# Where the adaLN rows stand on VectorE, which tiles have how many buffers, and when bank reads and residual loads are issued, in a hybrid RWKV-7 decoder block

## The chip, the cores and the metric

The kernel runs on one core of a Trainium2 chip. The core has five engines that run side by side, each with its own queue of instructions taken in order: TensorE (PE; its weight loads are listed apart as PEld) for matrix products, VectorE (DVE) and ScalarE (ACT) for elementwise work, GpSimd (POOL), and SyncE (SP), whose queue here issues all the transfers between device memory and on-chip memory. The metric is the device time of one execution in microseconds (us).

## The reference

One decoder layer on x of 512 tokens by 2048 features, in float32. The adaLN vector c gives six modulation rows of 2048 numbers each: shift, scale and gate for each of the two halves of the layer.

```python
c_act = jax.nn.silu(c)
mod = c_act @ w_ada[l] + b_ada[l]
sh1, sc1, gt1, sh2, sc2, gt2 = jnp.split(mod[:, None, :], N_MOD, axis=-1)
h = _rmsnorm(x, norm1_g[l]) * (1.0 + sc1) + sh1
p = h @ w_in[l]
y_rwkv = _rwkv7_mixer(p[..., :N_RWKV_COLS], ...)
y_pool = _pool_mixer(p[..., N_RWKV_COLS:], pool_w[l], pool_b[l], pool_scale[l])
mix = jnp.concatenate([y_rwkv, y_pool], axis=-1) @ w_out[l]
x = x + gt1 * mix
h = _rmsnorm(x, norm2_g[l]) * (1.0 + sc2) + sh2
x = x + gt2 * _conv_ffn(h, w_up[l], conv_w[l], conv_b[l], w_down[l])
return _rmsnorm(x, norm_f_g)
```

The RWKV-7 mixer first blends each token's projection with the one before it (`p + mu * (shift(p) - p)`), makes decay, in-context rate and gate from three small LoRA products, and then runs, for each of 16 heads of 64 features, a recurrence over the 512 tokens: the state S is decayed, corrected by a delta rule and read out. The result is normalised per head, gets a bonus term, and is multiplied by the gate g. The pooling mixer takes running means over windows of 2, 4, 8 and 16 tokens and a 256 by 256 product for each of its four groups.

## The kernel before, in words

All activations lie transposed, features on the 128 partitions and the 512 tokens along the free axis. A large product is made in three passes: weights and activations are each split into a high and a low half that TensorE can take at full rate (`split_weights`, lines 117 to 125: ScalarE writes `whi`, VectorE writes `wlo`; four buffers for the raw weights, three for each half), and high by high, high by low and low by high are added in PSUM (lines 128 to 130).

A framework orders the instructions when the program is built: it takes what is ready by an estimate of time, the block with the highest priority first, and the order of each engine's queue is then fixed. At run time an instruction waits for what it needs, and what stands behind it on its engine waits with it. `hp()` and `tc.high_priority` lift a block; everything else has the order of the program text. `in_step(op, other)` adds an edge without a semaphore: `op` is placed behind `other` in the planned order, and nothing waits at run time.

The stages that matter here, in order:

- First projection: adaLN rows 0 to 31 and the input projection of nine tiles (up to about 205 us). Eight banks of PSUM, `pf[0..7]`, hold the last eight of its results. `shift` (line 267) reads a bank twice: ScalarE scales it into a tile (line 268) and VectorE adds the neighbour token's share (line 269). `xwa` (the LoRA inputs for decay and rate) gets a tanh (line 282), `xg` (two tiles of gate input) a sigmoid and a split into halves (lines 288 to 295), and then five banks give r, k, v of the first heads. The pool of the eight banks is closed, and its banks go to the next stage's tiles, each as soon as its reader is done.
- Four quads (`NQ`), each of four heads, 64 tokens by 64 tokens in chunks of `C = 64`. `front(g)` (lines 406 to 460) makes decay and rate; `rest(g)` (from line 462) makes the scores of each chunk (lines 483 and 485, and 542 and 544), inverts the 16 by 16 diagonal blocks on VectorE after a round trip through device memory (lines 507 to 572, the last VectorE operation at 566), then widens the inverse in two levels (lines 586 to 605: product, mask `pm` at 591, product, sum into X at 599, product, sum into Y at 605), then runs the eight chunks of the recurrence one after the other (lines 620 to 650; R at 624 and 625), reads out y (line 668), normalises it (675 to 680) and applies the gate with weights loaded as `lg` and split into `gw` (lines 683 to 693).
- As filler between the quads' own steps stand the projections of the next quads' r, k and v (`win_some`: a product of 48 matmuls, then `shift` into a tile `spill` that goes to device memory, lines 703 to 711) and the pooling groups (`pool`, from line 312; its weights are loaded by `load_pw` into a tile of the tag `war`).
- adaLN rows 32 to 79, cut in two halves along the 2048 inputs: 96 rows of 128 by 1024 (`ada_rest`, lines 372 to 386). Each is a load of 512 KB into a tile `war` with two buffers (line 380) and one VectorE operation that multiplies by silu(c) and sums (line 381). 24 rows belong to each quad; each is placed in step with a filler product (`beats`, a list of the last matmul of each weight tile), spread evenly over the filler of that quad, and the last 24 over the first pass of w_out.
- w_out, first pass (lines 765 to 782): 14 of the 16 tiles of the mixers' output are loaded back (`mxl`, line 767, in the buffers of the raw weights), split, and multiplied for the first ten output tiles; the sums go to device memory as `part`. Then the stage's memory is given up.
- w_out, second pass (from line 866): the residual tiles `x2` are loaded, ten from `part` and six from x, all 16 in one loop ahead of the products (lines 867 to 870). For the first ten output tiles the last two mixer tiles are added; the other six are made whole, in two halves of the tokens. `residual` (line 821) scales by the gate, adds, and sums squares for the second norm.
- The MLP, the down projection and the final norm, which the change does not touch.

Of the kernel before, what the change touches and what calls it, by code (L numbers as in the profile page):

```python
# [11 lines left out]
F32 = mybir.dt.float32  # L12
# [6 lines left out]
P = 128  # L19
T = 512  # L20
# [44 lines left out]
def block_kernel(ctx, tc, a, out, stop=None, dbg=None):  # L65
# [121 lines left out]
    if True:  # L187
# [78 lines left out]
        if True:  # L266
# [15 lines left out]
            S.activation(xwa[0:64, :], xwa[0:64, :], AF.Tanh)  # L282
            xg = two(cell("X", "xg"))
            xgh = []
            for i in range(2):
                t = xg[:, i, :]
                shift(pf[1 + i], 25 + i, t)
                S.activation(t, t, AF.Sigmoid)
                hi = ra.tile([P, T], F32R, tag=f"xgh{i}", name=f"xgh{i}")
                S.copy(hi, t)  # L290
                xgh.append(hi)
            xg1h, xg2 = xgh
            xg1l = ra.tile([P, T], F32R, tag="xg1l", name="xg1l")
            V.tensor_tensor(xg1l, xg[:, 0, :], xg1h[:, :].bitcast(F32), op=ALU.subtract)
            V.tensor_tensor(xg2[64:96, :], xg[64:96, 1, :], xg2[64:96, :].bitcast(F32), op=ALU.subtract)

            RKV = ("R", "K", "V")
            rkv0 = [cell(RKV[i], "rkv"[i]) for i in range(3)]
            for i, (t, x, m) in enumerate(((0, 0, 0), (1, 0, 8), (2, 0, 16), (0, 1, 1), (1, 1, 9))):
                shift(pf[3 + i], m, two(rkv0[t])[:, x, :])  # L300
            ps0ctx.close()
# [10 lines left out]
    def pool(gi):  # L312
# [18 lines left out]
        for d in range(2):  # L331
            ps = mmtile()
            for i in range(2):
                pe = PE.matmul(ps, pw[:, i, d * P : (d + 1) * P], z[:, i, :], start=i == 0, stop=i == 1)
# [35 lines left out]
    modq = ra.tile([P, 2, 48], F32, tag="modq", name="modq")  # L370

    def ada_rest(n0, n1):
        b, at = len(beats) - first_beat[0], first_beat[0]
        for n in range(n0, n1):
# [4 lines left out]
            wa = ra.tile([P, 2 * T], F32, tag="war", name="war", bufs=2)  # L379
# [17 lines left out]
    def flat(t):  # L397
        return t[:, 0 : 2 * T]
# [7 lines left out]
    def front(g, rkv):  # L406
# [31 lines left out]
        V.tensor_sub(cs, cs, mid[:, :, :].to_broadcast([P, 2 * NK, C + 1]))  # L438
# [14 lines left out]
        V.tensor_scalar_max(flat(inv), wide(psn), 1e-24)  # L453
# [813 lines left out]
```

## Time and profile before

| | us |
|---|---|
| median of 3 runs | 2329.66 |
| lowest and highest run | 2323.95 and 2334.65 |
| the profiled execution | 2332.65 |
| its span, first to last instruction | 2330.9 |

The profile is of one execution. Its page gives the busy time of each engine, the span in slices, the chain of work that ended last, the costliest groups of instructions and the transfers. Other views group instructions by line or tile, list who waited for whom, count busy time within given stretches, or list instructions in order of time. In a line such as `L381 DVE ... war<-war,cq x96 | 116.9, 1220 | 47.3 <-DMA war<-ada 47.2` stand the source line, the engine, the output and inputs by the program's names, the count, the total busy time in us and the mean in ns, and then how long the engine stood idle just before, and for what.

### The profile page before, as it was taken

How to read it: one execution, taken by the hardware profiler on the slowest of the kernel's cores; microseconds unless marked ns; L12 is line 12 of the kernel's file. 1: busy time of each engine (PE TensorE's matmuls, PEld its weight loads, DVE VectorE, ACT ScalarE, POOL GpSimd, SP SyncE). 2: the span in 40 equal slices, each digit the busy share in tenths (PEclk: the TensorE clock that was granted, in tenths of full speed). 3: DMA queues.
4: the chain of work that ended last, by engine and by line, in shares of the span. 5: the costliest groups of instructions: out<-in, count | busy, mean ns of one | idle time of the engine just before them, and what ended most of it. 6: DMA issues, size and time to landing. Idle time of an engine off the chain costs nothing.

```text
span 2330.9 us, 41813 instructions
## 1 busy us (share of the span) xinstructions
PE 2202.7 (95%) x16306; PEld 1878.0 (81%) x16306; DVE 1512.6 (65%) x2536; ACT 925.9 (40%) x1551; POOL 403.3 (17%) x390
## 2 busy tenths in 40 slices
PE   7999898888879898999999999999999999999997
PEld 5776666565657798899999999999999788888887
DVE  7896767685865669776656666656666444464457
ACT  4435242332523255544344434443444333343333
POOL 0000000000000005634434333344343000000000
PEclk9999999999989999999999999999999999999999
DMA  9884556566655775433333333333333766666555
GB/s 348 301 307 132 164 181 184 166 202 197 209 177 171 266 224 166 149 108 119 123 109 123 109 115 112 110 117 122 109 122 105 232 202 200 198 199 205 163 165 177
DMA packets 197465, 401.41 MB, mean 172 GB/s; under 512 B 37521, under 2 KB 49553, under 8 KB 193041
## 3 DMA queue, kind: packets, MB, share of 16 engines
q1 hardware_dynamic: 197266, 398.73, 54.0%
q8 instruction: 128, 2.10, 0.4%
q14 instruction: 71, 0.58, 0.1%
HBM read 364.56 MB, written 34.09 MB: 171 GB/s over the span
## 4 chain that ended last, share of the span: by engine, by line
PE 60%; DVE 2%; DMA 2%; ACT 0%; issue 0%; SPq 0%; DVEq 0%; ACTq 0%
PE b L130 20%; PE b L128 20%; PE b L129 20%; DVE wlo L124 1%; DMA wraw<-wdn 1%; DMA wraw<-wout 1%; DVE hl L159 0%; DVE x L1089 0%; ACT whi L122 0%; DVE acc L819 0%; DMA ald<-actd 0%; DVE h L157 0%; DMA x<-part 0%; DMA x<-x2d 0%; DVE x L823 0%
## 5 line engine op out<-in xcount | busy, mean ns | idle before, releaser
L122 ACT CAST whi<-wraw 128x512 fp32r<-128x512 f32 (+1 forms) x594 | 360.4, 609 | 820.8 <-DMA wraw<-wup 254.8
L124 DVE TENSOR_TENSOR wlo<-wraw,whi 128x512 fp32r<-128x512 f32 (+1 forms) x578 | 406.5, 705 | 270.9 <-ACT whi L122 263.1
L128 PE MATMUL b<-ah,whi 128*128 128x512 f32 (+1 forms) x980 | 350.0, 357 | 8.2 <-ACT whi L122 7.3
L130 PE MATMUL b<-ah,wlo 128*128 128x512 f32 (+1 forms) x980 | 349.5, 357 | 6.0 <-DVE wlo L124 5.8
L129 PE MATMUL b<-al,whi 128*128 128x512 f32 (+1 forms) x980 | 348.7, 356 | 0.0
L130 PE MATMUL b<-hh,wlo 128*128 128x512 f32 (+1 forms) x640 | 237.8, 372 | 6.0 <-DVE wlo L124 5.8
L128 PE MATMUL b<-hh,whi 128*128 128x512 f32 (+1 forms) x640 | 238.2, 372 | 0.0
L129 PE MATMUL b<-hl,whi 128*128 128x512 f32 (+1 forms) x640 | 237.8, 372 | 0.0
L128 PEld LDWEIGHTS b<-ah,whi 128*128 128x128 f32 x980 | 186.0, 190 | 36.6 <-ACT whi L122 10.8
L130 PEld LDWEIGHTS b<-ah,wlo 128*128 128x128 f32 x980 | 186.0, 190 | 34.4 <-DVE wlo L124 7.7
L129 PEld LDWEIGHTS b<-al,whi 128*128 128x128 f32 x980 | 186.1, 190 | 26.0
L984 DVE TENSOR_TENSOR pl<-raw,ph 128x768 fp32r<-128x768 f32 x104 | 105.4, 1014 | 153.0 <-ACT ph L983 153.0
L128 PE MATMUL mm<-ah,whi 128*128 128x512 f32 x444 | 183.3, 413 | 10.1 <-ACT whi L122 10.1
L130 PE MATMUL mm<-ah,wlo 128*128 128x512 f32 x444 | 183.8, 415 | 3.2 <-DVE wlo L124 3.2
L129 PE MATMUL mm<-al,whi 128*128 128x512 f32 x444 | 182.4, 411 | 0.0
L972 POOL TENSOR_TENSOR sums<-sums,raw 128x256 f32<-128x256 f32 x104 | 107.5, 1033 | 417.0 <-DVE sl L984 411.1
L130 PE MATMUL b<-tk,sl 128*128 128x256 f32 x624 | 176.7, 283 | 0.0
L129 PE MATMUL b<-tk,sh 128*128 128x256 f32 x624 | 176.5, 283 | 0.0
L128 PE MATMUL b<-tk,sh 128*128 128x256 f32 x624 | 176.0, 282 | 0.0
L983 ACT CAST ph<-raw 128x768 fp32r<-128x768 f32 x104 | 86.3, 830 | 165.9 <-PE b L129 159.5
L381 DVE SCALAR_TENSOR_TENSOR war<-war,cq 128x1024 f32<-128x1024 f32 x96 | 116.9, 1220 | 47.3 <-DMA war<-ada 47.2
L971 POOL TENSOR_TENSOR sums<-raw 128x512 f32<-128x512 f32 x104 | 135.8, 1305 | 66.9 <-DMA raw<-wups 33.1
(277 smaller groups left out, 4699.8 us busy)
## 6 DMA issues: line engine op xcount, KB each, us to landing
raw<-wups SPq DMA_DIRECT2D x104, 512.0 KB, 3.5
war<-ada SPq DMA_DIRECT2D x96, 512.0 KB, 4.4
wraw<-wdn SPq DMA_DIRECT2D x192, 256.0 KB, 3.2
wraw<-wup SPq DMA_DIRECT2D x160, 256.0 KB, 3.6
wa<-ada SPq DMA_DIRECT2D x32, 1024.0 KB, 7.5
wraw<-win SPq DMA_DIRECT2D x108, 256.0 KB, 4.1
ald<-actd SPq DMA_DIRECT2D x88, 256.0 KB, 2.7
wraw<-wout SPq DMA_DIRECT2D x78, 256.0 KB, 4.2
```

The source lines that it names most:

```text
L122: mark[0] = S.copy(hi[:, 0:w], raw[:, 0:w]).ins
L124: mark[1] = eng.tensor_tensor(lo[:, 0:w], raw[:, 0:w], hi[:, 0:w].bitcast(F32), op=ALU.subtract).ins
L128: PE.matmul(ps, wh, xh, start=start, stop=False)
L129: PE.matmul(ps, wh, xl, start=False, stop=False)
L130: return PE.matmul(ps, wl, xh, start=False, stop=stop)
L381: op = V.scalar_tensor_tensor(wa, wa, 1.0, cq[0], op0=ALU.mult, op1=ALU.mult, accum_out=modq[:, kq, j : j + 1])
L971: G.tensor_tensor(sa, raw[:, 1:3, :], raw[:, 0:1, :].to_broadcast([P, 2, W2]), op=ALU.add)
L972: G.tensor_tensor(sb2[:, 0, :], sa[:, 0, :], raw[:, 2, :], op=ALU.add)
L983: act = S.copy(hi[:, sl, :], t)
L984: dve = V.tensor_tensor(lo[:, sl, :], t, hi[:, sl, :].bitcast(F32), op=ALU.subtract)
```

## The change

The 24 rows of a quad are no longer placed in step with filler products. Each quad now collects in a list `spots[g]` 25 of its own VectorE operations, some of them twice or four times, and `ada_rest` places one row behind each of the first 24: three in `front` (lines 438, 453 and 458), two behind the scores of line 485, two behind those of line 544, four behind the end of the block inversion (line 566), one behind each mask (line 591), one behind each of the seven R sums (line 625), two behind the sum of line 668, one behind line 677 and up to two behind line 680. The last 24 rows stand behind quad 3's operations. The tile `war` gets three buffers. `spill`, `lg` and R get one buffer in place of two, and the pool weights, loaded in two halves, take the tags `lg` and `gw`. The eight `shift`s come first, with the tanh behind the fourth; the sigmoids, their casts and the low halves come behind all eight. The loads of the residual tiles go into the loops, each behind the product that it belongs to.

```diff
             shift(pf[0], 24, xwa)
-            S.activation(xwa[0:64, :], xwa[0:64, :], AF.Tanh)
             xg = two(cell("X", "xg"))
...
+            for i in range(2):
+                shift(pf[1 + i], 25 + i, xg[:, i, :])
+            for i, (t, x, m) in enumerate(((0, 0, 0), (1, 0, 8), (2, 0, 16), (0, 1, 1), (1, 1, 9))):
+                shift(pf[3 + i], m, two(rkv0[t])[:, x, :])
+                if i == 0:
+                    S.activation(xwa[0:64, :], xwa[0:64, :], AF.Tanh)
+            ps0ctx.close()
+            xgh = [ra.tile([P, T], F32R, tag=f"xgh{i}", name=f"xgh{i}") for i in range(2)]
...
+            def sigmoids():
+                for i in range(2):
+                    S.activation(xg[:, i, :], xg[:, i, :], AF.Sigmoid)
+                    S.copy(xgh[i], xg[:, i, :])
+                V.tensor_tensor(xg1l, xg[:, 0, :], xg1h[:, :].bitcast(F32), op=ALU.subtract)
+                V.tensor_tensor(xg2[64:96, :], xg[64:96, 1, :], xg2[64:96, :].bitcast(F32), op=ALU.subtract)
+
+            sigmoids()
 
     def load_pw(gi):
-        t = ra.tile([P, 2 * T], F32, tag="war", name="pw", bufs=2)
-        pw = t[:, 0:T].rearrange("p (i d) -> p i d", i=2)
-        nc.sync.dma_start(pw, a["poolw"][gi, :, :, :])
+        pw = [ra.tile([P, 2, P], F32, tag="lg", name="pw"), ra.tile([P, 3, P], F32, tag="gw", name="pw")[:, 0:2, :]]
+        for i in range(2):
+            nc.sync.dma_start(pw[i], a["poolw"][gi, :, i, :].rearrange("p (d w) -> p d w", d=2))
         return pw
...
+    spots = [[] for _ in range(NQ)]
 
     def ada_rest(n0, n1):
-        b, at = len(beats) - first_beat[0], first_beat[0]
-        for n in range(n0, n1):
+        for n, spot in zip(range(n0, n1), spots[n0 // 24]):
             kq, j = divmod(n, 48)
...
-            wa = ra.tile([P, 2 * T], F32, tag="war", name="war", bufs=2)
+            wa = ra.tile([P, 2 * T], F32, tag="war", name="war", bufs=3)
             nc.sync.dma_start(wa, a["ada2"][kq, j, :, :])
             op = V.scalar_tensor_tensor(wa, wa, 1.0, cq[0], op0=ALU.mult, op1=ALU.mult,
                                         accum_out=modq[:, kq, j : j + 1])
-            i = at + (n - n0) * b // (n1 - n0)
-            if i < len(beats):
-                in_step(op, beats[i])
-        first_beat[0] = len(beats)
+            in_step(op, spot)
...
-        V.tensor_copy(xyl[:, 0, :, :], xyl[:, 1, :, :].rearrange("p i j -> p j i"))
+        dve = V.tensor_copy(xyl[:, 0, :, :], xyl[:, 1, :, :].rearrange("p i j -> p j i"))
+        spots[g] += [dve.ins] * 4
...
-            V.tensor_tensor(rows(pm), wide(ps).rearrange("p (s t) -> p s t", t=C),
+            dve = V.tensor_tensor(rows(pm), wide(ps).rearrange("p (s t) -> p s t", t=C),
                             mlev[:, lev : lev + 1, :].to_broadcast([P, 2 * NK, C]), op=ALU.mult)
+            spots[g].append(dve.ins)
...
-                R = ra.tile([P, 2, C], F32, tag="rc", name="rc", bufs=2)
-                V.tensor_add(R, pc[:, :, 0:C], xv[:, :, c, :])
+                R = ra.tile([P, 2, C], F32, tag="rc", name="rc")
+                dve = V.tensor_add(R, pc[:, :, 0:C], xv[:, :, c, :])
+                spots[g].append(dve.ins)
...
-            lw = ra.tile([P, 2, P], F32, tag="lg", name="lg", bufs=2)
+            lw = ra.tile([P, 2, P], F32, tag="lg", name="lg")
...
-            t = ra.tile([P, T], F32, tag="spill", name="spill", bufs=2)
+            t = ra.tile([P, T], F32, tag="spill", name="spill")
...
-    for f in range(KT):
+
+    def load_x2(f):
         t = rx.tile([P, T], F32, tag=f"x2_{f}", name=f"x2_{f}")
         nc.sync.dma_start(t, part[f] if f < NW else a["xT"][:, f, :])
         x2.append(t)
+
     for f in range(NW):
         ps = bank()
         project(ps, a["wout"][f, :, NM * P :], M[NM:])
+        load_x2(f)
         residual(f, ps, mod[:, 32 + f : 33 + f], acc, 0, T, f == 0)
 
     def out_half(hf, f, engs=(V,)):
         ps = bank()[:, 0:HT]
         project(ps, a["wout"][f, :, :], half(M, hf), engs=engs)
+        if hf == 0:
+            load_x2(f)
         residual(f, ps, mod[:, 32 + f : 33 + f], acc, hf * HT, (hf + 1) * HT, False)
```

More of the change, by code (lines that the diff above doesn't have):

```diff
@@ L281, in block_kernel @@
             shift(pf[0], 24, xwa)
-            S.activation(xwa[0:64, :], xwa[0:64, :], AF.Tanh)
             xg = two(cell("X", "xg"))
-            xgh = []
+            RKV = ("R", "K", "V")
+            rkv0 = [cell(RKV[i], "rkv"[i]) for i in range(3)]
             for i in range(2):
[L286 to L291, printed above, removed]
+                shift(pf[1 + i], 25 + i, xg[:, i, :])
@@ L295, in block_kernel @@
[L295 to L301, printed above, removed]
+            def sigmoids():
[4 more added lines that the diff above has]
+                V.tensor_tensor(xg2[64:96, :], xg[64:96, 1, :], xg2[64:96, :].bitcast(F32), op=ALU.subtract)
@@ L333, in pool @@
             for i in range(2):
-                pe = PE.matmul(ps, pw[:, i, d * P : (d + 1) * P], z[:, i, :], start=i == 0, stop=i == 1)
+                pe = PE.matmul(ps, pw[i][:, d, :], z[:, i, :], start=i == 0, stop=i == 1)
             j = gi * 2 + d
@@ L437, in front @@
         V.tensor_copy(mid, cs[:, :, C // 2 : C // 2 + 1])
-        V.tensor_sub(cs, cs, mid[:, :, :].to_broadcast([P, 2 * NK, C + 1]))
+        dve = V.tensor_sub(cs, cs, mid[:, :, :].to_broadcast([P, 2 * NK, C + 1]))
+        spots[g].append(dve.ins)
         ep = cell("EP", "ep")
@@ L452, in front @@
             PE.matmul(psn[:, x, :], bones, two(inv)[:, x, :], start=True, stop=True)
-        V.tensor_scalar_max(flat(inv), wide(psn), 1e-24)
+        dve = V.tensor_scalar_max(flat(inv), wide(psn), 1e-24)
+        spots[g].append(dve.ins)
         with tc.issue_after(act.ins):
@@ L459, in front @@
                                           op0=ALU.mult, op1=ALU.mult)
+        spots[g].append(norm.ins)
         return (al, ep, em, inv, fdec), norm
@@ L484, in scores @@
                                   arx[HS[h], x, 4 * hh + c, :, :], start=True, stop=True)
-                V.tensor_tensor(out[:, :, 4 * hh : 4 * hh + 4, :, :].rearrange("p x c w t -> p x c (w t)"),
+                dve = V.tensor_tensor(out[:, :, 4 * hh : 4 * hh + 4, :, :].rearrange("p x c w t -> p x c (w t)"),
                                 ps[:, :, :].rearrange("p x (c u) -> p x c u", c=4),
@@ L488, in scores @@
                                     [P, 2, 4, 2 * C]), op=ALU.mult)
-            return out
+            return out, dve
         def by_token(tag, src, mat):
@@ L499, in by_token @@
             return slab(t)
-        sb = scores("b", bt)
+        sb, dve = scores("b", bt)
+        spots[g] += [dve.ins] * 2
         dn = tc.dram_tile([2, 4, 2 * NK, 16, 16], F32, name=f"dn{g}")
@@ L543, in rest @@
                               arx[HS[h], x, 4 * hh + c, :, :], start=True, stop=True)
-            V.tensor_tensor(sk[:, :, 4 * hh : 4 * hh + 4, :, :].rearrange("p x c w t -> p x c (w t)"),
+            dve = V.tensor_tensor(sk[:, :, 4 * hh : 4 * hh + 4, :, :].rearrange("p x c w t -> p x c (w t)"),
                             ps[:, :, :].rearrange("p x (c u) -> p x c u", c=4),
@@ L547, in rest @@
                                 [P, 2, 4, 2 * C]), op=ALU.mult)
+        spots[g] += [dve.ins] * 2
         psb = batch()
@@ L590, in rest @@
             pm = cell("PM", "pm")
-            V.tensor_tensor(rows(pm), wide(ps).rearrange("p (s t) -> p s t", t=C),
+            dve = V.tensor_tensor(rows(pm), wide(ps).rearrange("p (s t) -> p s t", t=C),
                             mlev[:, lev : lev + 1, :].to_broadcast([P, 2 * NK, C]), op=ALU.mult)
+            spots[g].append(dve.ins)
             if lev == 0:
@@ L667, in rest @@
                     PE.matmul(o, ua[tk(x, h), x, c, :], sb[tk(x, h), x, c, 1, :], start=False, stop=c == NK - 1)
-        V.tensor_add(flat(y), flat(y), wide(ps))
+        dve = V.tensor_add(flat(y), flat(y), wide(ps))
+        spots[g] += [dve.ins] * 2
         yield
@@ L676, in rest @@
         S.activation(flat(rs), flat(rs), AF.Exp, scale=-0.5)
-        V.tensor_mul(flat(rs), flat(y), flat(rs))
+        dve = V.tensor_mul(flat(rs), flat(y), flat(rs))
+        spots[g].append(dve.ins)
         for x in range(2):
             S.activation(two(rs)[:, x, :], two(rs)[:, x, :], AF.Identity, bias=c2("lnb", x), scale=c2("lnw", x))
-        V.tensor_add(flat(rs), flat(rs), flat(bv))
+        dve = V.tensor_add(flat(rs), flat(rs), flat(bv))
+        spots[g] += [dve.ins] * 2
         pg = batch()
         for x in range(2):
-            lw = ra.tile([P, 2, P], F32, tag="lg", name="lg", bufs=2)
+            lw = ra.tile([P, 2, P], F32, tag="lg", name="lg")
             nc.sync.dma_start(lw, a["lora"][2 * g + x, :, 1:3, :])
@@ L700, in block_kernel @@
     sp, last_mix = {}, []
-    first_beat = [0]
     def win_some(pairs, which):
@@ L726, in block_kernel @@
     rkv = rkv0
-    first_beat[0] = len(beats)
     with hp():
```

2 lines of the change are left out of this document (1 added, 1 removed).

## The prediction, made before the change was run

> **What bounds the kernel now.** I read the page first, then the busy time by stretch of the middle part, the waits of TensorE, and at last the timeline around its longest idle stretches.
>
> ```profile
> span 2330.9 us, 41813 instructions
> PE 2202.7 (95%) x16306; PEld 1878.0 (81%) x16306; DVE 1512.6 (65%) x2536; ACT 925.9 (40%) x1551; POOL 403.3 (17%) x390
> L381 DVE SCALAR_TENSOR_TENSOR war<-war,cq 128x1024 f32<-128x1024 f32 x96 | 116.9, 1220 | 47.3 <-DMA war<-ada 47.2
> ```
>
> TensorE (PE) is busy 95% of the span, so all that a better order can win is its idle time, 2330.9 - 2202.7 = 128 us, and whatever runs at a reduced clock. The third line is the group that the change is about: the 96 adaLN rows cost VectorE (DVE) 1.22 us each, and VectorE stood idle 47.2 us in front of them because the row's load had not landed.
>
> ```profile
> core 0: us, PE busy (x) PEld busy (x) DVE busy (x) ACT busy (x) POOL busy (x), PEclk, DMA share, GB/s
> 200.00:240.00 40.00, 31.57 (x375) 22.26 (x377) 31.33 (x40) 28.27 (x40) 0.95 (x1) 0.96 0.26 75
> 240.00:345.00 105.00, 95.26 (x1199) 67.27 (x1192) 68.96 (x137) 38.34 (x67) 0.95 (x1) 0.98 0.56 169
> 345.00:470.00 125.00, 108.93 (x1492) 77.33 (x1491) 85.71 (x159) 42.93 (x72) 0.95 (x1) 0.97 0.60 182
> 470.00:610.00 140.00, 125.08 (x1534) 88.01 (x1533) 99.40 (x179) 51.97 (x86) 0.95 (x1) 0.95 0.63 190
> 610.00:735.00 125.00, 101.93 (x1449) 76.59 (x1448) 81.24 (x157) 39.66 (x72) 0.00 (x0) 0.90 0.58 181
> 735.00:796.00 61.00, 60.06 (x266) 49.44 (x265) 40.88 (x71) 15.38 (x29) 0.00 (x0) 1.00 0.78 252
> 796.00:820.00 24.00, 17.58 (x70) 13.64 (x71) 16.29 (x29) 10.20 (x20) 0.00 (x0) 0.86 0.82 281
> ```
>
> These stretches are the start of quad 0, quads 0 to 3, the first pass over w_out, and its second. Together TensorE is idle 620 - 540.42 = 79.6 us of the 128 here: this is the ceiling of the change. From 735 to 796 us it has 0.94 us idle, so taking rows away from there, as the change does, wins nothing by itself. The waits of TensorE name what it waits for:
>
> ```profile
> PE b L130 <- DVE wlo L124: 11.7, 10, 4.5
> PE mm L128 <- ACT whi L122: 10.1, 2, 9.8
> PE bt L588 <- DVE X L599: 8.7, 3, 3.7
> PE bt L656 <- DVE Y L605: 7.1, 4, 2.7
> PE bt L420 <- DVE r L269: 4.5, 1, 4.5
> PE bt L603 <- DVE pm L591: 2.3, 1, 2.3
> ```
>
> Columns: total us, times, longest. Lines 591, 599 and 605 are the chain that inverts a quad's triangular blocks: mask on VectorE, product on TensorE, sum on VectorE, twice over. Its three rows add up to 18.1 us. What stands in front of them on VectorE is seen in quad 1:
>
> ```profile
> 406.65 1.16 PE L597 MATMUL bt<-pm,Y 64*64 64x64 f32 x64
> 410.94 1.23 DVE L381 SCALAR_TENSOR_TENSOR war<-war,cq 128x1024 f32<-128x1024 f32 x1 [4.75 <-DMA war<-ada]
> ...
> 414.00 1.22 DVE L599 TENSOR_TENSOR X<-X,bt 128x1024 f32<-128x1024 f32 x1
> 415.27 1.98 PE L588 MATMUL bt<-X,sb 64*64 64x64 f32 x64 [3.66 <-DVE X L599]
> ```
>
> The product that X needs was done at 406.65 + 1.16 = 407.8. X starts at 414.00, 6.2 us later, because VectorE takes its queue in order and the row stands ahead, itself held 4.75 us by its own transfer (another row, left out here, follows it). Here the rows, which nobody waits for until the w_out stage, are on the critical path.
>
> **The change part by part.** All of it is summed against the profiled execution's own 2332.65 us (span 2330.9 and 1.75 around it). The median of the three runs, 2329.66, is 3.0 lower; that is taken off at the end.
>
> Eight shifts first:
>
> ```profile
> 204.66 1.28 ACT L288 ACT_TABLE_LOAD   x1
> 207.01 1.12 ACT L290 CAST xgh<-xg 128x512 fp32r<-128x512 f32 x2
> 211.20 0.18 PEld L421 LDWEIGHTS bt<-xwa,lw 64*64 64x64 f32 x1 [1.13 <-DVE v L269]
> ```
>
> ScalarE (ACT) spends 204.66 to 208.13 on a table load, two sigmoids and two casts before it empties the remaining banks. The change puts these 3.5 us behind; only tanh, with its own table load, remains ahead, behind the fourth shift. The first LoRA product waits for the fourth shift (the 4.5 us row), now read out before tanh: that wait goes whole. The next one waits for v, which stood behind all 3.5 us. Between 3.5 and 4.5 I take 3.7; the bounds are 0 (the moved sigmoids then hold up quad 0's own sigmoids) and 4.5.
>
> Rows behind the quads' own VectorE operations, three buffers. The work stays, 96 x 1.22 us and 96 transfers; places and buffers change.
>
> ```profile
> war<-ada SPq DMA_DIRECT2D x96, 512.0 KB, 4.4
> SPq L380 <- DVE war L381: 121.6, 50, 9.8
> 303.05 0.29 DVE L625 TENSOR_TENSOR rc<-ch,xv 128x128 f32<-128x128 f32 x1 [0.39 <-PE ch L623]
> 310.09 0.29 DVE L625 TENSOR_TENSOR rc<-ch,xv 128x128 f32<-128x128 f32 x1 [0.71 <-PE ch L623]
> ```
>
> A load lands 4.4 us after its issue (first row). A row behind the mask of line 591 runs while TensorE makes the product, 1.16 us at 406.65, if its data is there; with three buffers two more loads may be in flight while one row is worked on. Behind the R sums of the chain over time (two steps in 310.09 - 303.05 = 7.04 us) one row of 1.22 us per step of 3.5 leaves each load 7.0 us. Of the four behind line 566 the last has to wait for a buffer, but the quad's next operation on VectorE is a round trip through DRAM away. The second row is the load queue (SP) waiting for a row to give its buffer back, 121.6 us, with weight loads queued behind; it should fall, though where weights are buffered ahead that is hidden. Of the 18.1 us I take half, 9: mask and sums stay 1.2 us operations with a handover on each side, and the weights' low halves (line 124) stay in the same queue. Bounds: 0 and 18.1.
>
> Fewer idle stretches also mean less time at a lower clock (the number behind POOL):
>
> ```profile
> 290.00:300.00 10.00, 8.28 (x173) 6.18 (x171) 6.65 (x11) 1.80 (x3) 0.00 (x0) 0.87 0.61 200
> 410.00:420.00 10.00, 6.11 (x113) 5.37 (x114) 8.22 (x12) 0.72 (x1) 0.00 (x0) 0.66 0.64 205
> ```
>
> ```profile
> 283.33 0.27 PE L597 MATMUL bt<-pm,Y 64*64 64x64 f32 x2 [2.49 <-issue]
> 287.95 1.16 PE L588 MATMUL bt<-X,sb 64*64 64x64 f32 x64 [2.43 <-DVE X L599]
> ```
>
> Missing there, in the chains of quads 0 and 1: 1.3 + 3.4 = 4.7 us, so some 9.4 in four quads if TensorE were bound by its clock, which 64x64 products behind VectorE mostly are not. I take 3, bounds 0 and 9.4.
>
> The Trainium skill ("TensorE: Matmul & The Clock Gate", "Why this matters for your kernels") advises against idle gaps above about 3 us, because an idle window returns the array to half clock. This trace is stricter: the clock is down at 290 to 300 us, behind two gaps of 2.49 and 2.43 us. By the page's limit quad 0 would win no clock, and this term would be nearer 2 than 3.
>
> Quad 3's stall. TensorE waits once 9.8 us (the row of whi above) for the first w_out weights, which stand in SP's queue behind the loads of 14 mix tiles; these wait for buffers that VectorE empties:
>
> ```profile
> 659.18 0.79 PE L128 MATMUL mm<-ah,whi 128*128 128x512 f32 x1 [9.77 <-ACT whi L122]
> L152 DVE TENSOR_TENSOR al<-mxl,ah x14: 682/684/689, 625.5 to 657.9; 128x512 fp32r<-128x512 f32 x14
> L381 DVE SCALAR_TENSOR_TENSOR war<-war,cq x8: 1214/1222/1227, 623.2 to 650.6; 128x1024 f32<-128x1024 f32 x8
> ```
>
> Around these splits run 8 rows, 8 x 1.22 = 9.8 us. By the new places the stretch holds four, two behind line 485 and two behind line 544, so 4.9 us of VectorE come free. I take 4 of idle time, and 1 of clock, of which the stretch of quad 3 misses most (0.90); bounds 0 and 9.8.
>
> Residual loads spread:
>
> ```profile
> 801.86 0.75 DVE L823 SCALAR_TENSOR_TENSOR x<-b,mod,x 128x512 f32<-128x512 f32 x1 [0.88 <-DMA x<-part]
> 803.48 4.75 SPq L869 DMA_DIRECT2D x<-xT  x6
> 810.74 0.50 PE L130 MATMUL b<-ah,wlo 128*128 128x512 f32 x1 [4.54 <-DVE wlo L124]
> ```
>
> The residuals start in a row when their loads land, and a weight split that TensorE needs stands behind them: 4.54 us idle. At the same time six loads needed much later (f from 10) hold SP to 803.48 + 4.75 = 808.2. Spread, each tile's load comes between its own weights and the next ones. I take 3 of idle time and, as the clock is 0.86 here, 1 more. Bounds: 2 lost (a residual now waits for its load) and 6 won, as 796 to 820 us has 24 - 17.58 = 6.4 idle.
>
> Single buffers:
>
> ```profile
> lg<-lora SPq DMA_DIRECT2D x8, 128.0 KB, 3.0
> sp<-spill SPq DMA_DIRECT2D x18, 256.0 KB, 3.0
> ```
>
> The second gate load of each quad can go out only after the first is split, so it lands 3.0 us later, and its products stand in TensorE's order: 4 x 3.0 = 12 at worst, 0 where other products are placed between. I take 2. The spill tile is overwritten every 10.8 us at the soonest (48 products at 60.06 / 266 = 0.226 us, from the stretch 735 to 796), against a store of 3.0: nothing, while SP is not late by some 7 us. The R buffer costs nothing, since its sums form a chain. The pool weights, now four pairs of half tiles in the gate tags, make quad 2's second pool load wait for its first: 0.5, bounds 0 and 3. Rows now begin in front 0, where VectorE is busy 31.33 of 40 us: three rows, 3.7 us at worst; I take 1.
>
> Sum: won 3.7 + 9 + 3 + 5 + 4 = 24.7; lost 2 + 0.5 + 1 = 3.5. 2332.65 - 21.2 = 2311.45 for a run like the profiled one, 2308.5 as a median.
>
> **The rivals.** First, no difference that counts. A measurement of this kernel can tell about 0.5%, 11.6 us. The rows only change places: VectorE keeps its 1.22 us each, quads 1 to 3 have filler products in a fixed order, and what one gap gives another takes. Only the shifts and the tail pay: 2332.65 - 3.7 - 4 + 3.5 - 3.0 = 2325.5. For it: the three waits of the chain are only 18.1 of the 79.6 us, and the rest is not laid to rows by name. Against it: the 4.75 us wait in front of X has no other cause than the row.
>
> Second, slower: the gate tags become a valve in SP's queue. A load that waits for its single buffer holds all loads behind it, weights and rows alike. It decides if SP waits at line 684, or at the pool loads, for over 5 us at a time: weights have three buffers for their halves, of 12 x 0.226 = 2.7 us of products each, which covers some 8 us less 3.0 for the load. Then each quad loses its 3.0 us for gates and about 5 for weights, 4 x 8 = 32, and the half clock stays: 2332.65 + 32 - 7.7 - 3.0 = 2354. For it: SP already waits long for single places, 9.8 us at worst at line 380. Against it: gate loads are only eight, and the queue's places are planned with one buffer in mind.
>
> Third, more: chains, clock and the stall all go to their upper bounds in part, 3.7 + 14 + 5 + 9 + 6 - 2 = 35.7, giving 2294. That is the forecast's own lower end.
>
> **How the numbers follow.** The forecast, with its lower end, has 0.62, the first rival 0.26, the slower one 0.12. These are faster, same and slower as they stand: the forecast's 2308.5 lies 21 us below 2329.66, the edge being 2318. The range goes down to 2291, a little below the third case, and up past the first rival to 2334; the slower rival and the extremes, about 0.2, are left out.
>
> **What would show it.** Right: VectorE's idle time in front of rows falls from 47.2 us to under 20; the waits on X, Y and the masks from 18.1 to about 9; the wait of 4.5 us for line 269 is gone; the 9.8 us stall is about half; 796 to 820 us holds under 3.5 us idle. All 96 rows lie before about 740 us. Wrong: rows still wait for their loads, or X and Y for rows (places fixed, order not); SP waits in the gate and pool loads (second rival); or TensorE's idle time between 200 and 820 us stays near 79.6 with other names on it (first rival).

## The result, and the profile after

| | before | after |
|---|---|---|
| median of 6 runs, us | 2329.94 | 2309.99 |
| lowest and highest, us | 2323.95 and 2334.65 | 2307.79 and 2314.14 |
| the profiled execution, us | 2332.65 | 2309.01 |

The ratio is 0.9917, with a 95% interval of 0.9899 to 0.9935: 0.83% faster, 19.95 us. The forecast was 2308.5. The sum came out; not all of its terms did.

The profiled executions differ by 23.6 us, somewhat more than the medians. Their busy time, cut at the same events in both (the end of the last product of the first projection, the first product of the second pass over w_out, and the last of that pass), shows where. The columns are those of the prediction's stretches. First before:

```profile
205.40:796.00 590.60, 517.47 (x6277) 376.77 (x6277) 404.71 (x734) 211.48 (x357) 3.81 (x4) 0.96 0.59 182
796.00:890.60 94.60, 87.45 (x643) 82.70 (x644) 63.78 (x116) 49.46 (x92) 10.38 (x8) 0.96 0.76 238
```

The same stretches after, and the first 24 us of the second one:

```profile
203.66:776.55 572.89, 513.33 (x6276) 375.27 (x6277) 403.81 (x736) 212.56 (x357) 3.81 (x4) 0.96 0.60 187
776.60:869.20 92.60, 88.31 (x642) 82.41 (x643) 63.20 (x117) 49.69 (x92) 10.34 (x8) 0.98 0.77 244
776.60:800.60 24.00, 20.85 (x97) 16.40 (x98) 17.52 (x31) 11.46 (x22) 0.00 (x0) 0.93 0.77 256
```

Quads and first pass took 17.7 us less: TensorE's idle time went from 590.60 - 517.47 = 73.1 to 572.89 - 513.33 = 59.6, and the same products were busy 4.1 us less. The second pass took 2.0 less. The other 3.9 lie in stages that the change does not touch. The first projection, for one, ended at 205.4 and at 203.7, and between 199.3 and 206.5 in all the profiles of this document, though it is the same work in each. So a single profile carries a few us of drift in a stage, and 17.7 + 2.0 = 19.7 is to be set against the 19.95 of the medians.

The waits of TensorE in quads and first pass, after (total us, times, longest):

```profile
PE bt L593 <- DVE X L605: 8.8, 2, 5.4
PE bt L497 <- DVE sb L487: 7.6, 4, 3.4
PE mm L128 <- ACT whi L122: 6.0, 1, 6.0
PE bt L609 <- issue: 5.1, 2, 3.3
...
PE bt L452 <- ACT sg L423: 3.6, 1, 3.6
...
PE bt L609 <- DVE pm L596: 2.2, 1, 2.2
...
PE bt L663 <- DVE Y L611: 1.6, 4, 0.4
...
PE bt L485 <- DVE ar L477: 1.2, 1, 1.2
...
PE bt L419 <- DVE r L269: 0.7, 1, 0.7
```

Line numbers moved: X is summed at line 605 now, Y at 611, the mask stands at 596, a row is multiplied at 383 and loaded at 382. To be seen: Y's wait fell from 7.1 to 1.6 and the stall on whi from 10.1 to 6.0, but X's stayed (8.7 before), and a wait on `sg` is new. What holds X is in the order of time, in quad 1:

```profile
388.28 4.48 SPq L577 DMA_DIRECT2D X<-dxy  x8
...
401.31 0.96 SPq L382 DMA_DIRECT2D war<-ada  x2
401.35 1.16 PE L603 MATMUL bt<-pm,Y 64*64 64x64 f32 x64
...
407.38 1.23 DVE L383 SCALAR_TENSOR_TENSOR war<-war,cq 128x1024 f32<-128x1024 f32 x1 [6.23 <-DMA war<-ada]
408.53 1.22 DVE L605 TENSOR_TENSOR X<-X,bt 128x1024 f32<-128x1024 f32 x1
409.80 1.45 PE L593 MATMUL bt<-X,sb 64*64 64x64 f32 x44 [5.43 <-DVE X L605]
```

The row that runs behind the first mask waits 6.23 us for its load, and X stands behind the row. SP issued that load only at 401.31, though the three rows that ran behind the block inversion, from 385.9 to 390.0 us, had given back all three buffers more than 11 us before. In between SP's order has the eight small loads of the round trip (first line), weights, a spill store, and two gate loads, of which the second waits 2.8 us for the first to be split. VectorE waits ahead of rows less often than before (35 times, 47.2 us) but for longer each time:

```profile
DVE war L383 <- DMA war<-ada: 27.1, 10, 6.2
```

And SP still waits for a row to give its buffer back, while the gate and pool loads of the second rival hardly hold it:

```profile
SPq L382 <- DVE war L383: 117.9, 51, 7.9
...
SPq L694 <- DVE gw L698: 5.5, 2, 2.8
...
SPq L308 <- DVE gw L698: 6.6, 2, 3.9
```

### The profile page after: what moved, and what is told of

It is laid out like the page before. It is cut to its first block, busy times and chain, and to the rows that moved or that the text cites. A ratio compares the mean times of both kernels' runs of the same rounds, so it can differ in the third digit from the quotient of the medians.

```text
span 2307.2 us, 41832 instructions
## 1 busy us (share of the span) xinstructions
PE 2197.2 (95%) x16306; PEld 1874.6 (81%) x16306; DVE 1509.7 (65%) x2536; ACT 926.7 (40%) x1551; POOL 408.0 (18%) x390
## 4 chain that ended last, share of the span: by engine, by line
PE 54%; DMA 1%; DVE 1%; ACT 0%; issue 0%; SPq 0%; DVEq 0%; ACTq 0%
PE b L128 18%; PE b L129 18%; PE b L130 18%; DMA wraw<-wdn 1%; DVE x L1102 0%; DMA ald<-actd 0%; DMA x<-x2d 0%; DVE wlo L124 0%; ACT whi L122 0%; DVE x L831 0%; DVE al L152 0%; PE b L178 0%; ACT ah L151 0%; DVE acc L827 0%; DVE sl L997 0%
## 5 line engine op out<-in xcount | busy, mean ns | idle before, releaser
L130 PEld LDWEIGHTS b<-hh,wlo 128*128 128x128 f32 x640 | 120.6, 188 | 28.6 <-DVE wlo L124 7.6
```

Of the source, the lines that this page charges most:

```text
L130: return PE.matmul(ps, wl, xh, start=False, stop=stop)
```

## The experiments

The forecast's theory was that the new places keep rows out of TensorE's waits and that the third buffer has their data there in time, while the shifts and the residual loads pay a little each. The rivals were that places or buffers alone do it, that little of it matters, and that the single buffers cost something. So the first five kernels split the change. Ratios are to the kernel before, with 95% intervals; the letters in the expectations stand for the theories as they are told there.

### Each part alone

**e1_shifts** is the kernel before with the eight shifts first:

```diff
             shift(pf[0], 24, xwa)
-            S.activation(xwa[0:64, :], xwa[0:64, :], AF.Tanh)
...
+            for i in range(2):
+                shift(pf[1 + i], 25 + i, xg[:, i, :])
             for i, (t, x, m) in enumerate(((0, 0, 0), (1, 0, 8), (2, 0, 16), (0, 1, 1), (1, 1, 9))):
                 shift(pf[3 + i], m, two(rkv0[t])[:, x, :])
+                if i == 0:
+                    S.activation(xwa[0:64, :], xwa[0:64, :], AF.Tanh)
             ps0ctx.close()
...
+            sigmoids()
```

> The kernel before with the eight shifts first, and nothing else changed. Theory A (the prediction): the first LoRA products start some 5 us earlier and 3.7 us of it stay to the end, ratio about 0.998. Theory B (from the changed kernel's trace): the moved sigmoids and casts now stand on ScalarE ahead of quad 0's own sigmoids, TensorE waits 3.57 us for these, and the start of quad 0's scores is no earlier (231.75 us against 231.18); then the ratio is 1.000, within 1 us.

Measured: 2327.89 us, ratio 1.0001 [0.9985, 1.0016]. Its waits of TensorE at the start of quad 0:

```profile
PE bt L454 <- ACT sg L426: 3.6, 1, 3.6
...
PE bt L422 <- DVE r L269: 0.7, 1, 0.7
```

The 4.5 us wait for line 269 is nearly gone and 3.6 us of waiting for `sg` stand in its place. ScalarE's order of time in the changed kernel shows why:

```profile
206.42 1.28 ACT L298 ACT_TABLE_LOAD   x1
207.72 1.15 ACT L298 ACTIVATE xg<-xg 128x512 f32<-128x512 f32 x2
209.39 1.12 ACT L299 CAST xgh<-xg 128x512 fp32r<-128x512 f32 x2
211.45 1.25 ACT L423 ACTIVATE sg<-bt,vec 128x512 f32<-128x512 f32 x2
```

The sigmoids and casts that were put behind the shifts still stand ahead of quad 0's own sigmoids (line 423), which TensorE needs next. The work was moved from in front of one TensorE wait to in front of the next.

**e2_spread** is the kernel before with only the residual loads in the loops:

```diff
-    for f in range(KT):
+    def load_x2(f):
...
     for f in range(NW):
         ps = bank()
         project(ps, a["wout"][f, :, NM * P :], M[NM:])
+        load_x2(f)
         residual(f, ps, mod[:, 32 + f : 33 + f], acc, 0, T, f == 0)
```

> The kernel before with only the residual loads moved into the loops. Theory A: the gain is 4 us (3 of idle time, 1 of clock), ratio about 0.998. Theory B: the part from the first product of the second w_out pass to the end of that pass was 2.0 us shorter in the changed kernel, so about 2 us, 0.999. A loss of 1 to 2 us would mean that residuals now wait for their loads.

Measured: 2332.07 us, ratio 1.0004 [0.9985, 1.0023]. The first 24 us of its second pass, and the pass:

```profile
800.50:824.50 24.00, 19.93 (x90) 15.69 (x91) 17.41 (x31) 11.25 (x21) 0.00 (x0) 0.93 0.79 243
800.50:894.30 93.80, 88.11 (x643) 82.60 (x644) 63.03 (x117) 49.54 (x92) 10.35 (x8) 0.98 0.78 241
```

TensorE is idle 4.1 of the 24 us in place of 6.4, and the pass takes 93.80 in place of 94.60. The interval of the whole kernel is too wide to tell 1 or 2 us. All fourteen profiles together tell more: the pass takes 94.0 to 96.0 us in the six with the loads up front (mean 95.0) and 92.7 to 95.4 in the eight with the loads in the loops (mean 93.6). So the gain is about 1.4 us, a little under theory B.

**e3_rows** is the changed kernel without these two parts: the shifts and the residual loads are as before, the rows and all buffers as after.

> The kernel before with the rows' new places and the buffers for them, without the early shifts and with the residual loads up front. Theory A: 24.7 - 3.5 - 3.7 - 4 = 13.5 us won, ratio 0.994. Theory B: the shifts bring nothing and the loads 2, so the rows bring some 18 of the 20 us, ratio 0.992.

Measured: 2310.6 us, ratio 0.993 [0.9912, 0.9949]. By the medians that is the whole gain but for 0.6 us; by the ratios, each to runs of the kernel before that were made beside it, but for 3, and the two intervals overlap. The quads and the first pass, cut as above, take 572.4 us here and 572.9 in the changed kernel. So the rows with their buffers bring the gain there, between the two theories' ratios, and the shifts bring none of it. The next two kernels split it.

**e4_buffers** is the kernel before with the buffers of after; the rows stay in step with the filler products:

```diff
-        t = ra.tile([P, 2 * T], F32, tag="war", name="pw", bufs=2)
-        pw = t[:, 0:T].rearrange("p (i d) -> p i d", i=2)
-        nc.sync.dma_start(pw, a["poolw"][gi, :, :, :])
+        pw = [ra.tile([P, 2, P], F32, tag="lg", name="pw"), ra.tile([P, 3, P], F32, tag="gw", name="pw")[:, 0:2, :]]
+        for i in range(2):
+            nc.sync.dma_start(pw[i], a["poolw"][gi, :, i, :].rearrange("p (d w) -> p d w", d=2))
...
-            wa = ra.tile([P, 2 * T], F32, tag="war", name="war", bufs=2)
+            wa = ra.tile([P, 2 * T], F32, tag="war", name="war", bufs=3)
```

(`rc`, `lg` and `spill` lose their `bufs=2` as in the change.)

> The kernel before with three buffers for the rows, the single buffers that make room, and the pool weights in the gate tags; the rows still in step with filler products. Theory A (waits for the load are the cost): most of the 47.2 us that VectorE waits in front of rows goes and at least half of the rows' gain comes, ratio 0.996 or lower. Theory B (the places are the cost: a row stands in front of X and Y whenever it is there): under 0.999 is not reached. Rival of the single buffers: 1.005 or more.

Measured: 2330.55 us, ratio 1.0012 [0.9999, 1.0025]. VectorE now waits little for the rows' loads:

```profile
DVE war L381 <- DMA war<-ada: 14.6, 10, 6.7
```

TensorE's waits, though, have only changed their names:

```profile
PE mm L128 <- ACT whi L122: 10.8, 1, 10.8
PE bt L603 <- DVE pm L591: 6.8, 1, 6.8
...
PE bt L588 <- DVE X L599: 1.2, 1, 1.2
```

X's wait fell from 8.7 to 1.2, but rows that are in step with filler products fall in front of other operations: pm's wait went from 2.3 to 6.8, and the stall on whi stays. So early data alone is worth nothing here, and VectorE's idle time in front of rows, 14.6 us against the 27.1 of the changed kernel, does not measure the gain.

**e5_places** has the new places with two buffers for the rows, the pool weights again in the tag `war`, and two buffers elsewhere: the buffer lines of e4_buffers undone in e3_rows.

> The kernel before with the rows' new places alone: two buffers for the rows, two for spill, gate weights and R, pool weights in the rows' buffers, shifts and residual loads as before. Theory A (buffers and places each needed): VectorE waits more for loads than with three buffers (over 40 us) and the ratio is 0.997 to 1.000. Theory B (the places do it): 0.993 to 0.995, near the rows with their buffers.

Measured: 2339.62 us, ratio 1.005 [1.0032, 1.0067]: slower than before, which neither theory had forecast. VectorE's waits for row loads rise:

```profile
DVE war L381 <- DMA war<-ada: 56.3, 33, 6.9
```

Two views show the largest hole, VectorE's rows and SP's issues in quad 2:

```profile
484.85 1.22 DVE L381 SCALAR_TENSOR_TENSOR war<-war,cq 128x1024 f32<-128x1024 f32 x1
...
543.40 1.23 DVE L381 SCALAR_TENSOR_TENSOR war<-war,cq 128x1024 f32<-128x1024 f32 x1 [4.75 <-DMA war<-ada]
```

```profile
486.48 0.38 SPq L306 DMA_DIRECT2D pw<-poolw  x1
...
536.75 2.89 SPq L380 DMA_DIRECT2D war<-ada  x2
```

No row ran for 58 us: the two pool groups of quad 2 sit in the rows' two buffers, loaded at 468.2 and 486.48 and used from 522 us on, so the next row load could go out only at 536.75. In the kernel before the same two groups held the rows up for 29 us (no row between 516.3 and 545.3). The rows then pile up: 22 run between 543 and 604 us.

**e9_two_buffers** separates the two things that e5_places lacks. It is e3_rows with two buffers for the rows, but the pool weights stay out of them:

```diff
-            wa = ra.tile([P, 2 * T], F32, tag="war", name="war", bufs=3)
+            wa = ra.tile([P, 2 * T], F32, tag="war", name="war", bufs=2)
```

> The rows run (new places, pool weights in the gate tags, single buffers elsewhere) with the rows' buffers set back from three to two: against the rows run only the third buffer differs, against the run of the places alone above all that pool weights no longer sit in the rows' two buffers. Theory A (the third buffer is what the places need): near the places alone, 1.000 to 1.005. Theory C (the places alone lose because quad 2's two pool weights hold both buffers from 486 to 540 us and push the rows back by 58 us; the third buffer is a minor matter): near the rows run, 0.993 to 0.996.

Measured: 2317.54 us, ratio 0.9952 [0.9936, 0.9967]; VectorE waits for its rows' loads

```profile
DVE war L381 <- DMA war<-ada: 34.8, 17, 6.7
```

This is theory C. The third buffer is worth 2317.5 - 2310.6 = 7 us by the medians (5 by the ratios, whose intervals overlap), and the remaining 2339.6 - 2317.5 = 22 us come with the pool weights leaving the rows' buffers. `rc`, `lg` and `spill` have one buffer here and two in e5_places, and that part was not tried by itself; but the time is lost around the hole and behind it. Counted from the end of the first projection, e5_places is 2 us behind e9_two_buffers at the last R sum of quad 1, 8 at that of quad 2 and 19 at that of quad 3, and between 543 and 604 us only 13 rows run in e9_two_buffers.

The parts thus do not add up: buffers alone 0, places alone 11 us lost, both together 16 (by the ratio) to 19 (by the medians) won.

### What the rows cost at all, and two attempts to win more

**e7_norows** leaves out the loads and the operations of the 96 rows; modulation rows 32 to 79 are set to zero:

```diff
-            wa = ra.tile([P, 2 * T], F32, tag="war", name="war", bufs=3)
-            nc.sync.dma_start(wa, a["ada2"][kq, j, :, :])
-            op = V.scalar_tensor_tensor(wa, wa, 1.0, cq[0], op0=ALU.mult, op1=ALU.mult,
-                                        accum_out=modq[:, kq, j : j + 1])
-            in_step(op, spot)
+            V.memset(modq[:, kq, j : j + 1], 0.0)
```

**e6_noloads** leaves out only the loads; the operation reads silu(c) twice:

```diff
-            nc.sync.dma_start(wa, a["ada2"][kq, j, :, :])
-            op = V.scalar_tensor_tensor(wa, wa, 1.0, cq[0], op0=ALU.mult, op1=ALU.mult,
+            op = V.scalar_tensor_tensor(wa, cq[0], 1.0, cq[0], op0=ALU.mult, op1=ALU.mult,
```

> The changed kernel with the 96 rows left out, loads and operations (their sums are set to 0, so these modulation rows are not computed). The ceiling of anything that can be done with the rows' order. Theory A: nearly all of it is the loads, so within 4 us of the run without loads. Theory B: the 96 x 1.22 us of VectorE count by themselves, a further 8 us or more.

> The changed kernel with the rows' 96 loads left out: each row's VectorE operation stays in its place and reads the tile of silu(c), so the second to fifth modulation rows are not computed. It shows what waiting for the loads and their traffic still costs after the change. Theory A (the row behind the first mask still holds X by its load, TensorE idle 3.35 and 5.43 us in quads 0 and 1 and similar in the others): 12 to 18 us below the changed kernel, 0.984 to 0.987 against the kernel before. Theory B (TensorE is bound elsewhere): under 4 us below it, 0.990.

Measured: 2275.25 us without rows, ratio 0.9773 [0.9754, 0.9791]; 2285.97 us without loads, ratio 0.9818 [0.9801, 0.9836]. The busy time of the latter in the quads and the first pass:

```profile
203.51:749.80 546.29, 504.60 (x6277) 368.41 (x6277) 403.64 (x736) 212.50 (x357) 3.81 (x4) 0.98 0.36 107
```

VectorE does the same 736 operations there as in the changed kernel. Of the 34.7 us that the rows still cost in the changed kernel, 117 us of VectorE work account for 10.7 (theory B of the run without rows), and the loads for 24.0, more than either theory of the run without loads had. In the quads and first pass the profile without loads is 26.6 us shorter than that of the changed kernel: TensorE idles 41.7 us in place of 59.6, and the same products are busy 8.7 us less, at a granted clock of 0.98 in place of 0.96. More of what the rows still cost is in their transfers than in their operations.

**e8_nomask** takes the place behind the first mask out of the list, where the row that held X in the timeline above ran:

```diff
-            spots[g].append(dve.ins)
+            if lev:
+                spots[g].append(dve.ins)
```

> The changed kernel with no row behind the first mask of each quad (24 places remain; the seven R sums and the last places take one row each earlier). Theory A: the row there waits 3.5 to 6.2 us for its load in every quad and holds X; without it TensorE's wait on X falls from 8.8 us to under 3 and 5 to 10 us are won, 0.988 to 0.990 against the kernel before. Theory B: the late load only moves to the next row, behind the second mask or the first R sum, and holds Y or R there: no difference to the changed kernel, 0.992.

Measured: 2308.46 us, ratio 0.9915 [0.9898, 0.9932]: the same as the changed kernel. Its waits of TensorE:

```profile
PE bt L610 <- issue: 7.4, 4, 4.1
...
PE bt L593 <- issue: 3.5, 1, 3.5
PE mm L336 <- DVE spill L269: 3.2, 2, 1.8
...
PE bt L593 <- DVE X L606: 2.3, 1, 2.3
```

X's wait went from 8.8 to 2.3, but waits that the profile names "issue" rose from 5.1 and 0.3 to 7.4 and 3.5, and the one for `spill` from 0.6 to 3.2: 8.1 us more in these three, against the 6.5 taken away. Other waits fell and rose too. In all, TensorE idles 56.3 us in the quads and first pass in place of 59.6, and the same products are busy 516.1 in place of 513.3, so that the stretch takes 572.3 us and took 572.9. Theory B's time came, but not its way: neither Y nor R is waited for more. What holds TensorE in the "issue" rows is not shown by the trace and stays open.

**e11_sigmoids** puts the gate's sigmoids and casts behind quad 0's own sigmoids in the order of the program text, to win what the early shifts did not:

```diff
-            sigmoids()
...
+        if g == 0:
+            act = sigmoids()
```

> The changed kernel with the gate input's sigmoids and casts traced inside quad 0's front, behind its own sigmoids and ahead of the next table load. Theory B (the early shifts win nothing because the moved sigmoids hold quad 0's own): TensorE's wait of 3.57 us for the front's sigmoid is gone, quad 0's scores start 3 us earlier counted from the last product of the first projection, and 1 to 4 us stay, ratio 0.990 to 0.991. If the gain is swallowed again by a later wait of quad 0 (VectorE, 31 of 40 us busy there), no difference to the changed kernel, 0.992.

Measured: 2314.57 us, ratio 0.9935 [0.992, 0.995]. The wait on `sg` is gone, and the first LoRA product waits again:

```profile
PE bt L418 <- DVE r L269: 5.6, 1, 5.6
```

0.7 has become 5.6, because the edit did not do what it was meant to. In ScalarE's order of time the gate's sigmoids (line 298) run at 205.59, ahead of the bank reads that are left (from 209.08) and ahead of quad 0's own (line 422, at 215.64): the framework's order, not the text's, decides. That is in effect the order of the kernel before, with 18 table loads of 1.28 us on ScalarE in place of 14. So the order that was wanted was not tried. In the two orders that did run (before and e11_sigmoids; e1_shifts and the changed kernel) TensorE lost 4 to 6 us at this place. The ratio is above both theories', but the quads and first pass take 572.4 us, as in the changed kernel (572.9); the rest of the 4.6 us between the two medians lies in stages that are the same in both.

### Why the loads still cost 24 us

Two theories were left. One: SP, which waits 117.9 us at row loads, holds up the quads' own loads that stand behind them. The other: the bytes themselves, 96 times 512 KB, take the transfer engines from loads that a quad is waiting for.

**e10_own_queue** issues the row loads from GpSimd's queue, so that SP never waits for a row:

```diff
-            nc.sync.dma_start(wa, a["ada2"][kq, j, :, :])
+            nc.gpsimd.dma_start(wa, a["ada2"][kq, j, :, :])
```

> The changed kernel with the rows' loads issued from GpSimd's queue, idle in these stages, in place of SP's. Theory D (what the loads still cost, some 24 us by the run without loads, is their late place in SP's queue and SP's waiting for rows' buffers, 117.9 us, with weights behind): VectorE's wait for rows' loads falls from 27 us to under 8 and 10 to 20 us are won, 0.983 to 0.988 against the kernel before. Theory E (it is the traffic, 96 x 512 KB beside the weights): no change, 0.990 to 0.993. If GpSimd's queue itself is slower, or its clearing of X comes late behind row loads, slower than the changed kernel, 0.994 or more.

Measured: 2327.6 us, ratio 0.9987 [0.9976, 0.9999]: nearly all of the gain is gone. VectorE hardly waits for its rows any more (5.7 us), but TensorE does for something else:

```profile
PE bt L583 <- DMA X<-dxy: 16.7, 4, 8.0
```

The row of these loads in its view of transfers (count, KB each, median us from issue to landing):

```profile
X<-dxy SPq DMA_DIRECT2D x32, 16.0 KB, 5.9
```

X<-dxy are the small loads that bring the inverted blocks back, and a quad stands still until they land. In the changed kernel, with the row loads in SP's queue, they landed in 2.6 us:

```profile
war<-ada SPq DMA_DIRECT2D x96, 512.0 KB, 4.5
X<-dxy SPq DMA_DIRECT2D x32, 16.0 KB, 2.6
```

With SP free of the rows the kernel is slower. In SP's one order the row loads had stood behind the round trip's (the eight X<-dxy at 388.3, the rows' at 401.3 in quad 1, above). On a queue of their own nothing keeps them apart, and in quad 1 four of them go out just around the eight small ones (the first and the last of the four are shown):

```profile
395.42 0.53 POOL L382 DMA_DIRECT2D war<-ada  x1 [9.83 <-DVE war L383]
396.82 4.24 SPq L577 DMA_DIRECT2D X<-dxy  x8
401.03 0.53 POOL L382 DMA_DIRECT2D war<-ada  x1 [2.79 <-DVE war L383]
```

This new harm hides what SP's freedom may be worth, so this run alone does not settle the first theory; the next one does. Nor is the new queue like SP's in all else: the page lists its packets as `software_dynamic` and SP's as `hardware_dynamic`, and GpSimd spends 0.53 us on each issue. What a second queue of SP's kind would do was not tried. The Trainium skill ("DMA: Bandwidth & Descriptors", "Issuing engines are not separate DMA queues") says that transfers issued by different engines share the same 16 DMA engines, so that a second issuing engine saves only the time to issue. The trace fits the sharing, 2.6 us becoming 5.9 beside the other queue's 512 KB loads.

**e12_small_loads** keeps the queue, the count and the operations of the rows, but each load brings an eighth of the row's bytes, 64 KB, and the operation reads this eighth eight times over:

```diff
-            nc.sync.dma_start(wa, a["ada2"][kq, j, :, :])
+            nc.sync.dma_start(wa[:, 7 * P :], a["ada2"][kq, j, :, 0:P])
```

> The changed kernel with each of the rows' 96 loads cut to an eighth (64 KB in place of 512): the row's VectorE operation, its place and size stay, it reads the eighth over and over, so these modulation rows are not computed. Loads, buffers and the load queue's waits for them stay; only the traffic goes. Theory E (the loads cost by their traffic, beside the quads' own transfers): near the run without loads, 0.980 to 0.984. Theory D (they cost by their place in SP's queue and SP's waits for rows' buffers): near the changed kernel, 0.990 to 0.993. Between the two, the shares are read from where it falls: 24 us lie between the changed kernel (2310) and the run without loads (2286).

Measured: 2282.51 us, ratio 0.9802 [0.9784, 0.9821], as fast as without loads. SP and VectorE:

```profile
SPq L382 <- DVE war L384: 100.7, 55, 6.6
```

```profile
DVE war L384 <- DMA war<-ada: 2.1, 2, 1.3
```

SP waits for the rows' buffers almost as long as before, 100.7 us of 117.9, and the kernel is no slower than without row loads; of SP's share only quad 3's stall may be left, 4.6 us here and none without row loads. So the first theory falls as the main cause, and the 24 us hang on the bytes. Whether it is more the row's own landing (2.4 us for the small loads, 4.5 for the full ones) or the traffic beside other loads (X<-dxy lands in 2.0 us here and without any row loads, 2.6 beside the full ones) is not told apart; the planned order differs a little too, so a few us of the 27 may be the order's.

## Why the prediction was right, point by point

The step that failed is **eight shifts first**: "Between 3.5 and 4.5 I take 3.7" should have been its own lower bound, 0. The text named that bound's mechanism, the moved sigmoids holding up quad 0's own, and e1_shifts shows just this (3.6 us for `sg`). This could have been read from the trace of before: the sigmoids of line 288 and of quad 0's front stand in one queue, and ScalarE idles only 1.32 us ahead of the latter, too little to hide the 3.5 us that were moved there.

**The chain's waits**: 9 of 18.1 were forecast. X, Y and the masks (before 8.7, 7.1 and 2.3; after 8.8, 1.6 and 2.2) went to 12.6, so 5.5 were won, all of them at Y; the step was right in its way and too large in its size. A row behind a mask runs beside the product only "if its data is there", as the prediction put it; behind the first mask it wasn't, because three rows in a burst ahead of it use up the three buffers and SP's order refills them late. e8_nomask shows that curing this one place would not have paid.

**The clock**: 3, and 1 more with quad 3, were forecast. The same products were busy 4.1 us less in quads and first pass, but the granted clock of that stretch reads 0.96 before and after, so how much of it is the clock's is not shown. At the places named in quads 0 and 1 it did not rise: the changed kernel's 290 to 300 us read 0.83 (0.87 before), and 407 to 417 us, behind the wait of 5.43 us, 0.67 (0.66 before, at 410 to 420).

**Quad 3's stall** fell from 9.8 us to

```profile
641.87 0.80 PE L128 MATMUL mm<-ah,whi 128*128 128x512 f32 x1 [6.02 <-ACT whi L122]
```

3.8 of the 4 forecast, but the reason given does not carry it. Around the splits, up to the product that waits, five rows run (612.5 to 630.9 us), where four were forecast and eight ran before. But in e4_buffers, where the rows are still in step with filler products, it is five as well (626.8 to 636.4), and the stall is 10.8; in e3_rows it is five, and 6.4. So it is the new places that shorten it, and not the number of rows. What in them does so is not settled: SP waits 8.8 us at row loads around there before (600 to 660 us) and 1.6 after (590 to 645), but only 4.0 in e4_buffers (612 to 662) too. Where SP's queue has no row load at all, in e6_noloads and e10_own_queue, TensorE waits no more than 1.9 us at a time for these weights.

**Residual loads**: 4 forecast; the pass took 2.0 us less in the profile of after and 0.8 less in e2_spread, with 3.15 us idle in the first 24 (under 3.5 was named). Over all fourteen profiles it is 1.4 us (e2_spread). The term was two to three times too large.

**Single buffers**: 2.5 lost was forecast, and 1 more for rows in front 0, which no run shows apart. In the kernel's time nothing is seen of the buffers' 2.5 (e4_buffers has them all, at a ratio of 1.0012 [0.9999, 1.0025], and a third row buffer besides); in the trace one gate load adds up to 2.8 us to the lateness of the row load in front of X. SP waits 5.5 and 6.6 us at gate and pool loads in all, at most 3.9 at a time, so the slower rival, which needed over 5 at a time, did not come about. What the prediction missed is the other sign: with the pool weights moved to the gate's tags, at a price of 0.5 in the sum, the new places won; with them in the rows' buffers they lost (e5_places, e9_two_buffers).

**Not in the sum**: the waits for the scores' inputs and the pool's, before

```profile
PE bt L483 <- DVE ar L475: 6.2, 3, 3.4
...
PE mm L334 <- DVE spill L269: 4.2, 3, 1.8
```

became 1.2 and 0.6; the waits for `sb` at line 497 rose from 4.5 to 7.6 and the "issue" ones at line 609 from 2.5 to 5.1. A row stood directly in front of `ar` in only one of the three cases (quad 3, 629.55 us), so why these two fell stays open. Too much for the shifts, the chain and the residual loads, and nothing for these: the errors cancel. That the median came within 2 us of the forecast is in part luck.

Of **what would show it**, Y's wait, the stall, the residuals and the last row (723.8 us) came as named. The wait for line 269 went to 0.7, but came back as the one for `sg`; the chain's waits stayed above the 9 named, at 12.6. VectorE's idle time in front of rows did not fall as far either: 27.1 us in place of under 20, and e4_buffers with its 14.6 and no gain shows that it was the wrong sign to watch. The rival "no difference" falls with e3_rows' interval, though its doubt, that what one gap gives another takes, was right about the shifts.

## What to carry to other kernels

Before a buffer tag is shared by background work and something slow, look at how long the other tenant sits in it: two pool tiles in the rows' two buffers stopped the rows for 58 us, and that kernel lost 11 us where the one with the pool tiles elsewhere won 11 to 12. Places and buffers of background work are one edit; each alone gave nothing or less. When a moved operation frees one wait, read the next wait on the same engine's queue first: two orders of ScalarE's work at the start of quad 0 cost the same. And where a framework plans the order, look in the trace whether the order that was asked for is the one that ran (e11_sigmoids).

## What was not expected of the hardware

The 96 VectorE operations of the rows, 117 us of work, cost 10.7 us in the kernel's time, and their loads, which nobody but the rows needs, 24: hidden work cost more by its transfers than by its engine. SP waiting more than 100 us in all at the rows' buffers cost nothing that the kernel's time shows (e12_small_loads). And 512 KB loads issued from GpSimd's queue more than doubled the landing time of 16 KB loads on SP's, 2.6 us to 5.9.
